# A down projection in pairs of column blocks, two of eight units by seven products

## The chip, the cores and the metric

The kernel runs on one core of one Trainium2 chip. The metric is the time of one execution on the device in microseconds (us); the time of a kernel is the median of its runs. The engines are called by their names or as the profile does: TensorE (PE; its weight loads PEld), VectorE (DVE), ScalarE (ACT), GpSimd (POOL) and SyncE (SP), whose queue issues the weight loads.

## The reference, cut to what matters

One decoder layer on 256 tokens of width 2048, in float32. The part that the change touches is the SwiGLU block with a hidden width of 5632:

```python
def swiglu(h, w_gate, w_up, w_down):
    g = jnp.einsum('bsd,df->bsf', h, w_gate)
    u = jnp.einsum('bsd,df->bsf', h, w_up)
    return jnp.einsum('bsf,fd->bsd', jax.nn.silu(g) * u, w_down)

h = layer_norm(ALPHA * h + m, ln1_g[i], ln1_b[i])
f = swiglu(h, w_ffn_gate[i], w_ffn_up[i], w_ffn_down[i])
h = layer_norm(ALPHA * h + f, ln2_g[i], ln2_b[i])
```

A mixer (a linear recurrence beside attention) comes ahead of it, and a gated per-layer input behind it.

## The kernel before

**Arithmetic.** Every float32 operand is split into a high part, a cast to fp32r, and a low part, the rest. A block product is three matmuls: high by high, high by low, low by high. The activations are the stationary operand (128 features by 128 tokens), the weights are the moving operand (128 features by 512 columns), and the sum builds up in a PSUM bank of 128 tokens by 512 columns, one for each half `h` of the tokens.

**Weights.** The class `Stream` brings the weights in, in the fixed order of the list `srcs`. A unit is one load of 128 x 2048 floats. SP's queue loads it (`load`, three units ahead at most); ScalarE casts the high part of a half of it (`prepare_hi`, line 156); VectorE subtracts to get the low part (`prepare_lo`, line 147). The halves rotate through six buffers, so a cast waits until TensorE has used up the half six places before. `free` says that a half is used up; `tick`, called after every six matmuls or so, runs the steps of other jobs that are due (each job is a Python generator, one step to a tick) and then prepares at most one low and one high part. No scheduler reorders anything: each engine works in the order in which the program issues.

**SwiGLU.** `FPARTS` cuts the hidden width into three parts of 16, 16 and 12 tiles of 128 features. A part is four (or three) groups of gate and up (`gate_up`, four tiles each), which leave the transposed product in `hT`, and then the part's down projection, added to the residual `z`.

In `gate_up` a unit is two feature tiles of the input by four column tiles of both gate and up. The first six units take eight block products each. The last two (`SEVEN`) take seven by Strassen's scheme: besides the four accumulators `q` there are `p1`, `p6`, `p5` and `p7`, the stationary operands of some products are sums of activations (`xsum`, made once in `sums_of_x1`), and the moving ones are sums of weights, which VectorE makes in `add_up` (line 128). Such a unit has four halves to prepare, one of them half as wide. `finish` puts the products together, applies silu and writes `hT` over some 18 ticks, well into the stage behind it.

In the down projection of before a unit is four tiles of `hT` by one column block of 512 columns. Blocks 0 and 1 run together, unit by unit, in four accumulators (`two`); block 2 and then block 3 follow by themselves, in two accumulators each. `token_major` issues a unit (lines 270 to 272 are the three matmuls); `residuals` adds a finished accumulator to `z` (lines 681 and 683) as a job, one token half to a tick. PSUM has four banks for these accumulators (tag `mm`), two more with the tag `aux` and two with the tag `sc`.

Of the kernel before, what the change touches and what calls it, by code (L numbers as in the profile page):

```python
# [20 lines left out]
P = 128  # L21
D = 2048
S = 256
KT = D // P
# [24 lines left out]
NSM = 32 + 8 * 4 + 1 + 64  # L49
PAIRS = KT // 2  # L50
SEVEN = 2


class Stream:
# [5 lines left out]

    def __init__(self, nc, pool, srcs, after_load, sevens):
        self.nc, self.pool, self.srcs, self.after_load = nc, pool, srcs, after_load
        self.sevens = sevens
        self.order = [(n, j) for n in range(len(srcs)) for j in range(4 if n in sevens else 2)]
        self.place = {key: i for i, key in enumerate(self.order)}
        self.sums, self.sums_pool = {}, None
        self.loaded = self.released = self.his = self.los = 0
        self.freed = self.seen = 0  # L70
        self.w32, self.parts, self.jobs, self.spare = {}, {}, [], []
        self.unit = 0
        self.held = False
# [22 lines left out]
    def load(self):  # L96
        while self.loaded < min(max(self.released, FIRST) + BUFS, len(self.srcs)):
            n = self.loaded
            w = self.new_load()
            if isinstance(self.srcs[n], tuple):  # L100
                for i, src in enumerate(self.srcs[n]):
                    dst = w[:, i * 1024:(i + 1) * 1024].rearrange("p (f c) -> p f c", f=4)
                    self.nc.sync.dma_start(dst, src)
            else:
                for c in (slice(0, 1024), slice(1024, 2048)) if n == FIRST else (slice(0, 2048),):
                    self.nc.sync.dma_start(w[:, c], self.srcs[n][:, c])
            if n in self.after_load:
                self.after_load[n]()

    def blocks(self, n):  # L110

        return self.w32[n].rearrange("p (g f k c) -> p g f k c", g=2, f=4, k=2)

    def source(self, i):

        n, j = self.order[i]
        if n in self.sevens and j:
            if j == 1:
                return self.blocks(n)[:, 1, :, 1, :], 512
            return self.sums[n][:, (j - 2) * 1024:(j - 1) * 1024], 1024  # L120
        return self.w32[n][:, j * 1024:j * 1024 + 1024], 1024

    def shaped(self, t, src, cols):
        return t[:, :cols].rearrange("p (f c) -> p f c", f=4) if cols == 512 else t

    def add_up(self, n, j):

        add = lambda out, a, b: self.nc.vector.tensor_tensor(out, a, b, ALU.add)
        b = self.blocks(n)
        if j == 0:  # L130
            self.sums[n] = self.sums_pool.tile([P, 2048], F32, tag="T", name="sums", bufs=2)
        t = self.sums[n].rearrange("p (i f c) -> p i f c", i=4, f=4)
        if j == 0:
            w = self.w32[n]
            diagonal = bass.AP(w.tensor, w.offset, [w.ap[0], [1024 + P, 2], [2 * P, 4], [1, P]])
            add(t[:, 0:2], diagonal, b[:, 1, :, 0, :].unsqueeze(1).broadcast_to([P, 2, 4, P]))
        else:
            t1, t2, t4 = t[:, 0], t[:, 2], t[:, 3]
            add(t2, t1, b[:, 1, :, 1, :])
            add(t4, t2, b[:, 0, :, 1, :])  # L140

    def prepare_lo(self):
        n, j = self.order[self.los]
        wh, wl = self.parts[n, j]
        src, cols = self.source(self.los)
        wh, wl = (self.shaped(t, src, cols) for t in (wh, wl))
        self.nc.vector.tensor_tensor(wl, src, wh.bitcast(F32), ALU.subtract)  # L147
        self.released += j == 1
        self.los += 1
        self.load()  # L150

    def prepare_hi(self):
        n, j = self.order[self.his]
        src, cols = self.source(self.his)
        wh, wl = self.new_half()
        self.nc.scalar.copy(self.shaped(wh, src, cols), src)  # L156
        if n in self.sevens and j < 2:
            self.add_up(n, j)

# [41 lines left out]
def tile_hybrid_layer(ctx: ExitStack, tc: tile.TileContext, t: dict):  # L201
# [14 lines left out]
    srcs += [t["w_out"][blk, kq] for blk, kq in OUT01]  # L216
    srcs += [t["w_out"][blk, kq] for blk in (2, 3) for kq in range(4)]
    srcs += [t["w_pp"][u] for u in range(2)]
    sevens = set()
    for f0, nf in FPARTS:  # L220
        for f in range(f0, f0 + nf, 4):
            sevens.update(range(len(srcs) + PAIRS - SEVEN, len(srcs) + PAIRS))
            srcs += [tuple(t[w][f:f + 4, :, 2 * P * j:2 * P * (j + 1)].rearrange("f p c -> p f c")
                           for w in ("w_gate", "w_up")) for j in range(PAIRS)]
        srcs += [t["w_down"][f0 // 4 + kq, blk] for kq in range(nf // 4) for blk in range(2)]
        srcs += [t["w_down"][f0 // 4 + kq, blk] for blk in range(2, 4) for kq in range(nf // 4)]
    srcs += [t["w_pg"][blk, kq] for blk in range(4) for kq in range(4)]
    after_load = {}
    st = Stream(nc, wp, srcs, after_load, sevens)

    def bank(name):
        return pm.tile([P, 512], F32, tag="mm", name=name)

    def aux(name):
        return pa.tile([P, 512], F32, tag="aux", name=name, bufs=2)
# [560 lines left out]
    x1 = act.tile([P, KT, 2 * S], F32R, tag="B", name="x1")  # L796
    xsum = []

    def sums_of_x1():

        xsum.append(late.tile([P, SEVEN, 4, 2, P], F32R, tag="gb", name="xsum"))
        work = act.tile([P, 2 * SEVEN * 512], F32, tag="A", name="work")
        x, sums = work[:, :SEVEN * 512], work[:, SEVEN * 512:]
        ks = slice(KT - 2 * SEVEN, KT)
        nc.vector.tensor_tensor(x.rearrange("p (k s) -> p k s", s=S), x1[:, ks, :S].bitcast(F32),
                                x1[:, ks, S:].bitcast(F32), ALU.add)
        yield
        a11, a21, a12, a22 = (x.rearrange("p (m i c) -> p m i c", i=4, c=P)[:, :, i, :] for i in range(4))  # L810
        s1, s3, s2, s4 = (sums.rearrange("p (m i c) -> p m i c", i=4, c=P)[:, :, i, :] for i in range(4))
        nc.vector.tensor_tensor(s1, a22, a21, ALU.subtract)
        nc.vector.tensor_tensor(s3, a11, a21, ALU.subtract)
        yield
        nc.vector.scalar_tensor_tensor(s2, s1, -1.0, a11, ALU.mult, ALU.subtract)
        nc.vector.tensor_tensor(s4, a12, s2, ALU.add)
        yield
        sums = sums.rearrange("p (n c) -> p n c", c=P)
        hi, lo = (xsum[0].rearrange("p m i a c -> p (m i) a c")[:, :, a, :] for a in range(2))
        nc.scalar.copy(hi, sums)  # L820
        yield
        nc.vector.tensor_tensor(lo, sums, hi.bitcast(F32), ALU.subtract)

    ps = [bank("ops") for _ in range(2)]
    for kq in range(2):
# [8 lines left out]

    def product(ps, a, w, first, last):

        out = ps.rearrange("p (f c) -> p f c", c=P)
        nc.tensor.matmul(out, a[0], w[0], start=first, stop=False)  # L838
        nc.tensor.matmul(out, a[0], w[1], start=False, stop=False)  # L839
        nc.tensor.matmul(out, a[1], w[0], start=False, stop=last)  # L840

    def operand(n, j, i):

        parts = st.half(n, j)
        if n in st.sevens and j:
            return [w[:, i * 512:(i + 1) * 512].rearrange("p (f c) -> p f c", c=P) for w in parts]
        return [w.rearrange("p (f k c) -> p f k c", f=4, k=2)[:, :, i, :] for w in parts]

    def gate_up(hT, i0):
# [46 lines left out]
    def finish(hT, i0, q, p1, p6, p5, p7):  # L896
# [34 lines left out]
        for h, g in enumerate((g0, g1)):  # L931
            tp = aux("tp")
            for i in range(4):
                nc.tensor.transpose(tp[:, i * P:(i + 1) * P], g[:, i * P:(i + 1) * P], ident)
            yield
            tp = tp.rearrange("p (a b) -> p a b", b=P)
            hi, lo = (hT[:, i0:i0 + 4, o + h * P:o + (h + 1) * P] for o in (0, S))
            nc.scalar.copy(hi, tp)
            yield
            nc.vector.tensor_tensor(lo, tp, hi.bitcast(F32), ALU.subtract)  # L940

    for part, (f0, nf) in enumerate(FPARTS):
        hT = None
        for i0 in range(0, nf, 4):
            hT = gate_up(hT, i0)
        nq = nf // 4
        end = part == len(FPARTS) - 1
        if end:
            gb = load_gb(2)
        two = [[bank("dps") for _ in range(2)] for _ in range(2)]  # L950
        for kq in range(nq):
            for blk in range(2):
# [187 lines left out]
```

## Time and profile before

| | |
|---|---|
| runs | 1183.46 us median of 3 (1183.11 to 1183.65) |
| profiled execution | 1183.25 us, of which the span of the trace is 1181.4 us |
| granted TensorE clock, mean | 0.996 |
| part 0: gate and up, then down projection | down from 530.0 to 618.7 us of the span |
| part 1: down projection | 790.3 to 878.9 us |

Times in the profile count from the start of the span. A line of the timeline gives the start, the duration and the instruction, and, in brackets, how long its engine stood idle in front of it and what ended that. The names are those of the program's tiles (`dps` is an accumulator of the down projection, `gu` and `p` those of gate and up, `wh` and `wl` high and low parts of weights).

### The profile page before, as it was taken

What the parts mean: (1) busy time and instruction counts of PE and PEld (TensorE: products, weight loads), DVE (VectorE), ACT (ScalarE), POOL (GpSimd) and SP (SyncE); (2) the same over time, 40 slices, a digit from 0 to 9 for tenths busy, and PEclk for the clock granted to TensorE, in tenths of its full rate; (3) what the DMA queues carried; (4) which work ended last, traced back from release to release, by engine and by line L of the source; (5) the groups of instructions that cost most, each with busy time, mean ns of one, the idle gap of its engine ahead of it and who ended that gap; (6) DMA issues with size and microseconds to landing.
All of it is one profiled execution on the core that took longest, in us unless ns stands there. A gap on an engine that the chain in (4) does not pass through costs nothing.

```text
span 1181.4 us, 14679 instructions
## 1 busy us (share of the span) xinstructions
PE 1163.0 (98%) x5576; PEld 967.3 (82%) x5576; DVE 871.7 (74%) x1126; ACT 629.1 (53%) x905; POOL 36.7 (3%) x64
## 2 busy tenths in 40 slices
PE   9999999999999999999999999999999999999995
PEld 6888888888888888888888888888888888877885
DVE  6965987775669877876555887885556887766877
ACT  6767566664356655654333664664334664535540
POOL 0000000001010000000000000000000000002001
PEclk9999999999999999999999999999999999999998
DMA  9766554547638557546565655655564755755741
GB/s 331 264 219 211 170 179 151 178 151 268 267 127 295 184 182 246 180 173 218 187 205 178 214 170 187 214 189 203 189 203 152 234 185 178 287 179 221 296 158 72
DMA packets 119703, 238.99 MB, mean 202 GB/s; under 512 B 5904, under 2 KB 100024, under 8 KB 103632
## 3 DMA queue, kind: packets, MB, share of 16 engines
q1 hardware_dynamic: 116208, 221.52, 54.7%
q0 software_dynamic: 3424, 16.53, 3.7%
q8 instruction: 44, 0.72, 0.2%
q14 instruction: 27, 0.22, 0.1%
HBM read 233.82 MB, written 5.78 MB: 203 GB/s over the span
## 4 chain that ended last, share of the span: by engine, by line
PE 95%; DVE 2%; ACT 1%; POOL 1%; DMA 0%; issue 0%; SPq 0%; DVEq 0%; POOLq 0%; ACTq 0%
PE gu L838 11%; PE gu L840 11%; PE gu L839 11%; PE dps L270 6%; PE dps L272 6%; PE dps L271 6%; PE q L244 3%; PE k L244 3%; PE yg L244 3%; PE ops L270 2%; PE ops L272 2%; PE ops L271 2%; PE xr L244 2%; PE gps L271 2%; PE gps L270 2%; PE gps L272 2%
## 5 line engine op out<-in xcount | busy, mean ns | idle before, releaser
L147 DVE TENSOR_TENSOR wl<-w,wh 128x1024 fp32r<-128x1024 f32 (+1 forms) x404 | 478.8, 1192 | 174.9 <-ACT wh L156 173.3
L156 ACT CAST wh<-w 128x1024 fp32r<-128x1024 f32 (+1 forms) x404 | 413.8, 1031 | 315.3 <-PE dps L272 120.2
L838 PE MATMUL gu<-wh,x 128*128 128x512 f32 x572 | 224.4, 392 | 0.0
L840 PE MATMUL gu<-wh,x 128*128 128x512 f32 x572 | 222.7, 389 | 0.0
L839 PE MATMUL gu<-wl,x 128*128 128x512 f32 x572 | 222.7, 389 | 0.0
L270 PE MATMUL dps<-wh,hT 128*128 128x512 f32 x352 | 138.0, 392 | 1.4 <-DVE z L683 1.1
L272 PE MATMUL dps<-wh,hT 128*128 128x512 f32 x352 | 137.1, 389 | 0.0
L271 PE MATMUL dps<-wl,hT 128*128 128x512 f32 x352 | 137.0, 389 | 0.0
L840 PEld LDWEIGHTS gu<-wh,x 128*128 128x128 f32 x572 | 107.4, 188 | 22.7
L838 PEld LDWEIGHTS gu<-wh,x 128*128 128x128 f32 x572 | 107.4, 188 | 21.8
L839 PEld LDWEIGHTS gu<-wl,x 128*128 128x128 f32 x572 | 107.5, 188 | 21.8
L147 DVE TENSOR_TENSOR wl<-sums,wh 128x1024 fp32r<-128x1024 f32 x44 | 52.9, 1224 | 49.5 <-ACT wh L156 49.5
L270 PEld LDWEIGHTS dps<-wh,hT 128*128 128x128 f32 x352 | 66.1, 188 | 16.4 <-issue 2.3
L272 PEld LDWEIGHTS dps<-wh,hT 128*128 128x128 f32 x352 | 66.1, 188 | 13.8
L271 PEld LDWEIGHTS dps<-wl,hT 128*128 128x128 f32 x352 | 66.1, 188 | 13.4
L156 ACT CAST wh<-sums 128x1024 fp32r<-128x1024 f32 x44 | 45.2, 1051 | 50.0 <-PE gu L840 41.9
L270 PE MATMUL ops<-wh,mhl 128*128 128x512 f32 x128 | 50.4, 394 | 0.0
L271 PE MATMUL ops<-wl,mhl 128*128 128x512 f32 x128 | 49.9, 390 | 0.0
L272 PE MATMUL ops<-wh,mhl 128*128 128x512 f32 x128 | 49.9, 390 | 0.0
L244 PE MATMUL xr<-xhl,wh 128*128 128x512 f32 x128 | 45.9, 401 | 1.6 <-ACT wh L76 1.6
L244 PE MATMUL q<-xhl,wh 128*128 128x512 f32 x128 | 47.3, 406 | 0.0
L244 PE MATMUL k<-xhl,wh 128*128 128x512 f32 x128 | 46.0, 400 | 0.0
(250 smaller groups left out, 1771.4 us busy)
## 6 DMA issues: line engine op xcount, KB each, us to landing
w<-in_w_gate SPq DMA_DIRECT2D x88, 512.0 KB, 3.7
w<-in_w_up SPq DMA_DIRECT2D x88, 512.0 KB, 4.8
w<-in_w_down SPq DMA_DIRECT2D x44, 1024.0 KB, 4.8
w<-in_w_a SPq DMA_DIRECT2D x28, 1024.0 KB, 4.9
w<-in_w_out SPq DMA_DIRECT2D x16, 1024.0 KB, 4.9
w<-in_w_pg SPq DMA_DIRECT2D x16, 1024.0 KB, 4.9
w<-in_w_v SPq DMA_DIRECT2D x8, 1024.0 KB, 4.9
gb<-in_ln_g POOLq DMA_DIRECT2D x3, 1024.0 KB, 5.2
```

The lines of the kernel that those rows point to most:

```text
L147: self.nc.vector.tensor_tensor(wl, src, wh.bitcast(F32), ALU.subtract)
L156: self.nc.scalar.copy(self.shaped(wh, src, cols), src)
L244: nc.tensor.matmul(ps, wh[:, c], xhl[:, k, :], start=(k == 0), stop=False)
L270: nc.tensor.matmul(ps, ah, wh[:, c], start=first, stop=False)
L271: nc.tensor.matmul(ps, ah, wl[:, c], start=False, stop=False)
L272: nc.tensor.matmul(ps, al, wh[:, c], start=False, stop=last)
L838: nc.tensor.matmul(out, a[0], w[0], start=first, stop=False)
L839: nc.tensor.matmul(out, a[0], w[1], start=False, stop=False)
L840: nc.tensor.matmul(out, a[1], w[0], start=False, stop=last)
```

## The change

In parts 0 and 1 the down projection goes by pairs of column blocks. A unit is now two tiles of `hT` (`m` counts these pairs of tiles) by two column blocks, 8 units to a pair, in the order of `DOWN`. Kind "N" is a unit of eight block products, kind "S" one of seven. The four accumulators of a pair (two token halves by two column blocks) run through all eight units, and each is read into `z` right after its own last product. The S units need sums of `hT`'s first four tiles, made behind the first group of gate and up of the part (`sums_of`), and their weights' sums (`add_up`); `p1`, `p6`, `p5` and `p7` run over both S units of a pair, and `products_to_z` adds them to `z` in nine additions. Weights come as two loads of 512 KB to a unit. Part 2 is as before.

```diff
+DOWN = ((("N", 2), ("N", 3), ("N", 4), ("N", 5), ("S", 0), ("N", 6), ("S", 1), ("N", 7)),
+        (("N", 2), ("N", 3), ("N", 4), ("S", 0), ("N", 5), ("N", 6), ("S", 1), ("N", 7)))
...
+        if nf == KT:
+            for pair, order in enumerate(DOWN):
+                for kind, m in order:
+                    if kind == "S":
+                        sevens.add(len(srcs))
+                    plain.add(len(srcs))
+                    srcs.append(tuple(t["w_down"][f0 // 4 + m // 2, 2 * pair + i, :, m % 2 * 1024:m % 2 * 1024 + 1024]
+                                      for i in range(2)))
+            continue
...
-        xsum.append(late.tile([P, SEVEN, 4, 2, P], F32R, tag="gb", name="xsum"))
+        xsum.append(late.tile([P, 2 * SEVEN, 4, 2, P], F32R, tag="gb", name="xsum"))
...
             nc.vector.tensor_tensor(lo, tp, hi.bitcast(F32), ALU.subtract)
+        if i0 == 0 and paired:
+            yield
+            yield from sums_of(hT, 0, late.tile([P, 2048], F32, tag="T", name="work", bufs=2), SEVEN)
+
+    def down_pair(hT, pair, order, scale):
+
+        n0 = st.take(len(order))
+        q = [[bank("dps") for _ in range(2)] for _ in range(2)]
+        places = [i for i, (kind, _) in enumerate(order) if kind == "S"]
+        for pos, (kind, m) in enumerate(order):
+            n, end = n0 + pos, pos == len(order) - 1
+            first, last = pos == places[0], pos == places[-1]
+            def x(h, i):
+                return [hT[:, 2 * m + i, o + h * P:o + (h + 1) * P] for o in (0, S)]
+            def sx(i):
+                return [xsum[0][:, SEVEN + m, i, a, :] for a in range(2)]
+            if kind == "N":
+                for g in range(2):
+                    for h in range(2):
+                        for i in range(2):
+                            product(q[h][g], x(h, i), operand(n, g, i), pos + i == 0, end and i == 1)
+                        if end:
+                            residual(h, 2 * pair + g, q[h][g], scale)
+                        st.free(h)
+                        st.tick()
+                continue
+            if first:
+                p1, p6 = aux("p1"), aux("p6")
+                both = pa.tile([P, 2, 512], F32, tag="sc", name="p57")
+                p5, p7 = both[:, 0, :], both[:, 1, :]
+            product(q[0][0], x(0, 1), operand(n, 0, 1), False, False)
+            product(p1, x(0, 0), operand(n, 0, 0), first, last)
+            st.free()
+            st.tick()
+            product(q[0][1], sx(3), operand(n, 1, 0), False, False)
+            st.free()
+            product(p5, sx(0), operand(n, 2, 0), first, last)
+            st.tick()
+            product(p7, sx(1), operand(n, 2, 1), first, last)
+            st.free()
+            product(q[1][0], x(1, 1), operand(n, 3, 1), False, False)
+            st.tick()
+            product(p6, sx(2), operand(n, 3, 0), first, last)
+            if last:
+                st.start(products_to_z(pair, p1, p6, p5, p7))
+            st.free()
+            st.tick()
+
+    def products_to_z(pair, p1, p6, p5, p7):
+
+
+        add = lambda out, a, b, op=ALU.add: nc.vector.tensor_tensor(out, a, b, op)
+        c1, u2, u3, u4 = (tmp(i) for i in ("c1", "u2", "u3", "u4"))
+        nc.scalar.copy(c1, p1)
+        yield
+        add(u2, p6, c1)
+        yield
+        add(u3, p7, u2)
+        yield
+        add(u2, p5, u2)
+        yield
+        add(u4, p5, u3)
+        yield 2
+        for h, g, u, op in ((0, 0, c1, ALU.add), (1, 0, u3, ALU.add), (0, 1, u2, ALU.subtract),
+                            (1, 1, u4, ALU.subtract)):
+            c = slice((2 * pair + g) * 512, (2 * pair + g + 1) * 512)
+            add(z[:, h, c], z[:, h, c], u, op)
+            yield
...
+        if paired:
+            for pair, order in enumerate(DOWN):
+                down_pair(hT, pair, order, part == 0)
+            continue
         two = [[bank("dps") for _ in range(2)] for _ in range(2)]
```

`sums_of` is the body of the old `sums_of_x1` with its source, its place in `xsum` and its work buffer as arguments: one addition of 1024 columns, four of 256, a cast and a subtraction of 1024. In `Stream`, the units in `plain` are read as two column blocks of two tiles of 512 columns in a row, where those of gate and up have four pieces of 128 columns.

## Rows read from the trace of the kernel before

**Rows 1.** The page: span, then busy us (share) and instructions of each engine.
```profile
span 1181.4 us, 14679 instructions
...
PE 1163.0 (98%) x5576; PEld 967.3 (82%) x5576; DVE 871.7 (74%) x1126; ACT 629.1 (53%) x905; POOL 36.7 (3%) x64
```

**Rows 2.** TensorE's waits, whole span: for whom, us, times, longest.
```profile
PE dps L270 <- DVE z L683: 1.1, 3, 0.4
PE dps L270 <- DVE z L681: 0.4, 1, 0.4
```

**Rows 3.** TensorE's timeline, part 0's down projection: start us, us, instruction.
```profile
530.01 0.39 PE L270 MATMUL dps<-wh,hT 128*128 128x512 f32 x1
...
543.38 0.39 PE L272 MATMUL dps<-wh,hT 128*128 128x512 f32 x1
```

**Rows 4.** The same timeline at the step to the third column block.
```profile
574.30 0.39 PE L272 MATMUL dps<-wh,hT 128*128 128x512 f32 x1
575.06 0.47 PE L270 MATMUL dps<-wh,hT 128*128 128x512 f32 x1 [0.38 <-DVE z L681]
575.37 0.40 PE L271 MATMUL dps<-wl,hT 128*128 128x512 f32 x1
```

**Rows 5.** The same step in part 1.
```profile
834.56 0.39 PE L272 MATMUL dps<-wh,hT 128*128 128x512 f32 x1
835.33 0.47 PE L270 MATMUL dps<-wh,hT 128*128 128x512 f32 x1 [0.38 <-DVE z L683]
```

**Rows 6.** VectorE's timeline at the step of rows 4.
```profile
573.09 1.23 DVE L147 TENSOR_TENSOR wl<-w,wh 128x1024 fp32r<-128x1024 f32 x1 [1.50 <-ACT wh L156]
574.23 1.28 DVE L681 SCALAR_TENSOR_TENSOR z<-z,dps 128x512 f32<-128x512 f32 x2
```

**Rows 7.** Busy time by stretch: a gate and up group, part 0's down projection.
```profile
core 0: us, PE busy (x) PEld busy (x) DVE busy (x) ACT busy (x) POOL busy (x), PEclk, DMA share, GB/s
444.40:487.50 43.10, 43.10 (x195) 35.70 (x194) 34.67 (x39) 23.97 (x30) 0.00 (x0) 1.00 0.59 194
530.00:618.67 88.67, 88.29 (x393) 72.80 (x392) 51.83 (x52) 37.37 (x39) 0.00 (x0) 1.00 0.59 206
```

**Rows 8.** Groups by shape on VectorE: count | busy us, mean ns | idle before.
```profile
L147 DVE TENSOR_TENSOR wl<-w,wh 128x1024 fp32r<-128x1024 f32 x382 | 463.8, 1222 | 174.9 <-ACT wh L156 173.3
...
L128 DVE TENSOR_TENSOR sums<-sums,w 128x512 f32<-128x512 f32 x44 | 30.3, 689 | 0.8
...
L899 DVE TENSOR_TENSOR u<-p,u 128x512 f32<-128x512 f32 x44 | 30.2, 686 | 0.4
...
L128 DVE TENSOR_TENSOR sums<-w 128x1024 f32<-128x1024 f32 x22 | 26.8, 1219 | 0.7 <-DMA w<-in_w_up 0.7
...
L147 DVE TENSOR_TENSOR wl<-w,wh 128x512 fp32r<-128x512 f32 x22 | 15.1, 684 | 0.0
...
L683 DVE TENSOR_TENSOR z<-z,dps 128x512 f32<-128x512 f32 x16 | 10.5, 679 | 3.1 <-PE dps L272 3.1
...
L77 DVE TENSOR_TENSOR wl<-w,wh 128x256 fp32r<-128x256 f32 x21 | 7.7, 421 | 0.4 <-ACT wh L76 0.4
```

**Rows 9.** TensorE's timeline, the last two units of a gate and up group.
```profile
477.34 0.39 PE L838 MATMUL gu<-wh,x 128*128 128x512 f32 x1
...
484.14 0.39 PE L838 MATMUL p<-wh,xsum 128*128 128x512 f32 x1
...
486.86 0.39 PE L838 MATMUL gu<-wh,x 128*128 128x512 f32 x1
```

**Rows 10.** VectorE's timeline in the same group, subtractions from the sums.
```profile
470.51 1.23 DVE L147 TENSOR_TENSOR wl<-sums,wh 128x1024 fp32r<-128x1024 f32 x1 [2.32 <-ACT wh L156]
...
480.03 2.36 DVE L147 TENSOR_TENSOR wl<-sums,wh 128x1024 fp32r<-128x1024 f32 x2 [0.92 <-ACT wh L156]
```

**Rows 11.** The page: DMA issues, count, KB each, median us to landing.
```profile
w<-in_w_gate SPq DMA_DIRECT2D x88, 512.0 KB, 3.7
...
w<-in_w_down SPq DMA_DIRECT2D x44, 1024.0 KB, 4.8
```

More of the change, by code (lines that the diff above doesn't have):

```diff
@@ L51, with __init__ @@
 SEVEN = 2
+DOWN = ((("N", 2), ("N", 3), ("N", 4), ("N", 5), ("S", 0), ("N", 6), ("S", 1), ("N", 7)),
+        (("N", 2), ("N", 3), ("N", 4), ("S", 0), ("N", 5), ("N", 6), ("S", 1), ("N", 7)))
 class Stream:
-    def __init__(self, nc, pool, srcs, after_load, sevens):
+    def __init__(self, nc, pool, srcs, after_load, sevens, plain):
+        self.plain = plain
         self.nc, self.pool, self.srcs, self.after_load = nc, pool, srcs, after_load
@@ L101, in load @@
                 for i, src in enumerate(self.srcs[n]):
-                    dst = w[:, i * 1024:(i + 1) * 1024].rearrange("p (f c) -> p f c", f=4)
+                    dst = w[:, i * 1024:(i + 1) * 1024]
+                    dst = dst if n in self.plain else dst.rearrange("p (f c) -> p f c", f=4)
                     self.nc.sync.dma_start(dst, src)
@@ L110, in blocks @@
     def blocks(self, n):
-        return self.w32[n].rearrange("p (g f k c) -> p g f k c", g=2, f=4, k=2)
+        if n in self.plain:
+            return self.w32[n].rearrange("p (g k c) -> p g k c", g=2, k=2)
+        return self.w32[n].rearrange("p (g f k c) -> p g k f c", g=2, f=4, k=2)
     def source(self, i):
@@ L118, in source, with shaped @@
             if j == 1:
-                return self.blocks(n)[:, 1, :, 1, :], 512
+                return self.blocks(n)[:, 1, 1], 512
             return self.sums[n][:, (j - 2) * 1024:(j - 1) * 1024], 1024
         return self.w32[n][:, j * 1024:j * 1024 + 1024], 1024
-    def shaped(self, t, src, cols):
-        return t[:, :cols].rearrange("p (f c) -> p f c", f=4) if cols == 512 else t
+    def shaped(self, t, n, cols):
+        if cols == 1024 or n in self.plain:
+            return t[:, :cols]
+        return t[:, :cols].rearrange("p (f c) -> p f c", f=4)
     def add_up(self, n, j):
@@ L131, in add_up @@
             self.sums[n] = self.sums_pool.tile([P, 2048], F32, tag="T", name="sums", bufs=2)
-        t = self.sums[n].rearrange("p (i f c) -> p i f c", i=4, f=4)
+        w = self.w32[n]
+        if n in self.plain:
+            t = self.sums[n].rearrange("p (i c) -> p i c", i=4)
+            diagonal = bass.AP(w.tensor, w.offset, [w.ap[0], [1024 + 512, 2], [1, 512]])
+            b12 = b[:, 1, 0].unsqueeze(1).broadcast_to([P, 2, 512])
+        else:
+            t = self.sums[n].rearrange("p (i f c) -> p i f c", i=4, f=4)
+            diagonal = bass.AP(w.tensor, w.offset, [w.ap[0], [1024 + P, 2], [2 * P, 4], [1, P]])
+            b12 = b[:, 1, 0].unsqueeze(1).broadcast_to([P, 2, 4, P])
         if j == 0:
-            w = self.w32[n]
-            diagonal = bass.AP(w.tensor, w.offset, [w.ap[0], [1024 + P, 2], [2 * P, 4], [1, P]])
-            add(t[:, 0:2], diagonal, b[:, 1, :, 0, :].unsqueeze(1).broadcast_to([P, 2, 4, P]))
+            add(t[:, 0:2], diagonal, b12)
         else:
             t1, t2, t4 = t[:, 0], t[:, 2], t[:, 3]
-            add(t2, t1, b[:, 1, :, 1, :])
-            add(t4, t2, b[:, 0, :, 1, :])
+            add(t2, t1, b[:, 1, 1])
+            add(t4, t2, b[:, 0, 1])
     def prepare_lo(self):
@@ L145, in prepare_lo @@
         src, cols = self.source(self.los)
-        wh, wl = (self.shaped(t, src, cols) for t in (wh, wl))
+        wh, wl = (self.shaped(t, n, cols) for t in (wh, wl))
         self.nc.vector.tensor_tensor(wl, src, wh.bitcast(F32), ALU.subtract)
@@ L155, in prepare_hi @@
         wh, wl = self.new_half()
-        self.nc.scalar.copy(self.shaped(wh, src, cols), src)
+        self.nc.scalar.copy(self.shaped(wh, n, cols), src)
         if n in self.sevens and j < 2:
@@ L218, in tile_hybrid_layer @@
     srcs += [t["w_pp"][u] for u in range(2)]
-    sevens = set()
+    sevens, plain = set(), set()
     for f0, nf in FPARTS:
@@ L228, in tile_hybrid_layer @@
     after_load = {}
-    st = Stream(nc, wp, srcs, after_load, sevens)
+    st = Stream(nc, wp, srcs, after_load, sevens, plain)
     def bank(name):
@@ L797, in tile_hybrid_layer, with sums_of @@
     xsum = []
-    def sums_of_x1():
-        xsum.append(late.tile([P, SEVEN, 4, 2, P], F32R, tag="gb", name="xsum"))
-        work = act.tile([P, 2 * SEVEN * 512], F32, tag="A", name="work")
+    def sums_of(xt, k0, work, m0):
         x, sums = work[:, :SEVEN * 512], work[:, SEVEN * 512:]
-        ks = slice(KT - 2 * SEVEN, KT)
-        nc.vector.tensor_tensor(x.rearrange("p (k s) -> p k s", s=S), x1[:, ks, :S].bitcast(F32),
-                                x1[:, ks, S:].bitcast(F32), ALU.add)
+        ks = slice(k0, k0 + 2 * SEVEN)
+        nc.vector.tensor_tensor(x.rearrange("p (k s) -> p k s", s=S), xt[:, ks, :S].bitcast(F32),
+                                xt[:, ks, S:].bitcast(F32), ALU.add)
         yield
@@ L818, in sums_of_x1 @@
         sums = sums.rearrange("p (n c) -> p n c", c=P)
-        hi, lo = (xsum[0].rearrange("p m i a c -> p (m i) a c")[:, :, a, :] for a in range(2))
+        hi, lo = (xsum[0][:, m0:m0 + SEVEN].rearrange("p m i a c -> p (m i) a c")[:, :, a, :] for a in range(2))
         nc.scalar.copy(hi, sums)
@@ L822, in sums_of_x1 @@
         nc.vector.tensor_tensor(lo, sums, hi.bitcast(F32), ALU.subtract)
+    def sums_of_x1():
+        xsum.append(late.tile([P, 2 * SEVEN, 4, 2, P], F32R, tag="gb", name="xsum"))
+        work = act.tile([P, 2 * SEVEN * 512], F32, tag="A", name="work")
+        yield from sums_of(x1, KT - 2 * SEVEN, work, 0)
     ps = [bank("ops") for _ in range(2)]
@@ L835, in product @@
     def product(ps, a, w, first, last):
-        out = ps.rearrange("p (f c) -> p f c", c=P)
+        out = ps.rearrange("p (f c) -> p f c", c=P) if len(w[0].shape) == 3 else ps
         nc.tensor.matmul(out, a[0], w[0], start=first, stop=False)
@@ L844, in operand @@
         parts = st.half(n, j)
-        if n in st.sevens and j:
-            return [w[:, i * 512:(i + 1) * 512].rearrange("p (f c) -> p f c", c=P) for w in parts]
+        if n in st.plain or n in st.sevens and j:
+            return [w[:, i * 512:(i + 1) * 512] for w in parts]
         return [w.rearrange("p (f k c) -> p f k c", f=4, k=2)[:, :, i, :] for w in parts]
@@ L942, in tile_hybrid_layer @@
     for part, (f0, nf) in enumerate(FPARTS):
-        hT = None
+        hT, paired = None, nf == KT
         for i0 in range(0, nf, 4):
```

## The prediction, as it was made

> **What bounds the kernel now.** I read the page's busy shares first [rows 1]: TensorE is at work in 98% of the span, VectorE in 74%. A busy share alone doesn't say that TensorE sets the pace, because its matmul records overlap, so I went to TensorE's own waits next. There are hardly any: in the down projections of the three parts together it waited 1.5 us in four places, each time for VectorE to take a sum out of an accumulator [rows 2]. The stages of part 0 and part 1 run at the granted clock 1.00, the upper level, 2.4 GHz [rows 7]. So in the stretch that the change touches the end is set by how many matmuls TensorE is given, and by nothing else except two short waits.
>
> The price of one matmul has to be read from starts, not from durations. In part 0's down projection the first matmul starts at 530.01 and the sixtieth at 543.38 [rows 3]: 13.37 us over 59 steps, 0.2266 us each. A record's own duration is 0.39 us; whoever multiplies by that counts the overlap twice and gets a gain 1.7 times too large.
>
> The two waits are at the step from the second to the third block of columns. In part 0 the last matmul of block 1 starts at 574.30, the next at 575.06 and the one behind it at 575.37 [rows 4]: 1.07 us for two steps that should take 0.45, so 0.62 lost. Part 1 shows the same gap, 834.56 to 835.33 [rows 5], and I put it at the same 0.62. The reason stands on VectorE: the readout of block 0's accumulator (z, line 681) comes to its turn at 574.23, straight behind a 1.23 us weight subtraction [rows 6], though block 0 itself had been finished a whole unit earlier.
>
> **The change part by part.**
>
> *Removed: matmuls.* A unit is 2 tiles of the 16 by 2 column blocks by 2 token halves: 8 block products of 3 matmuls, 24, or 5.44 us. An S unit has 7 products, 21 matmuls, 4.76 us. Eight S units (2 of 8 in each of 2 pairs of 2 parts) save 24 matmuls: 24 x 0.2266 = 5.44 us. That the seven products keep the same step is seen in gate and up, where the scheme is in use: the last two units of a group, 42 matmuls, run from 477.34 to 486.86 [rows 9], 9.52 us, again 0.2267 each, with the four extra accumulators in play. The operand of a plain unit is 512 columns in a row, as that of the old down projection.
>
> By the Trainium skill ("TensorE: Matmul & The Clock Gate", Back-to-back issue gap) a stream of weight loads and matmuls of 512 columns sustains about 131 ns for one, and an isolated one about 216 ns. By these the saving would be an estimated 3.1 or 5.2 us; the row shows 0.2266 us over 59 steps without a break, and the row decides.
>
> *Moved: the readout of accumulators.* Four accumulators now run through a whole pair and each is read right behind its own last product, in program order ahead of that step's weight preparation. The next user of the same accumulator comes 18 matmuls, 4.08 us, after its last product. A readout takes 0.68 us [rows 8]. I take the two waits of 0.62 as gone: 1.24 us. Lower bound of this term: they stay or come back at all four pair ends (rival B). Upper bound: there is nothing more than these to win here.
>
> *Added on VectorE, per S unit.* Subtractions: three of 1024 columns and one of 512 in place of two of 1024, 3 x 1.22 + 0.68 = 4.35 against 2.44. Sums: one of 1.22 and two of 0.69, 2.60. Together 6.95 us where a plain unit has 2.44 [rows 8]. *Per pair:* nine 512-column additions from the four extra accumulators into z, 9 x 0.69 = 6.2, of the kind of line 899. *Per part:* the sums of hT in the second group of gate and up: 1.22 + 4 x 0.42 + 1.22 = 4.1, the 256-column ones by the row of line 77. For the down projection of one part that is 4 x 4.51 + 2 x 6.2 = 30.4 on top of 51.8 [rows 7]: 82.2 of the 85.3 us that the stage will then last (88.67 less 12 x 0.2266 and 0.62). This is 96%, and the one thing that speaks against the change.
>
> I cost it at nothing, and the cover is this. Six halves of weights are prepared ahead of TensorE, so work on VectorE delays nothing until that lead is eaten. In program order the densest stretch of a pair is from one step into the first S unit to two steps behind its end: subtractions and sums for the second S unit, 1.22 + 1.22 + 1.22 + 1.38 + 0.68 + 1.22 + 1.22 = 8.2 us at full durations, while TensorE spends 6.1 us. VectorE comes out 2 us late, but the first of these halves is wanted a whole plain unit, 5.4 us, after the S unit ends, and the last 3.4 us later still. In pair 1 the additions into z fall together with the first S unit's sums (about 8.5 us against 6.8), and that unit is still one and a half plain units away. In gate and up two S units stand side by side, a harder case: there VectorE idled 2.32 us in front of the first of these subtractions, and the last two, done by 482.4 [rows 10], were first wanted at 484.14 [rows 9], 1.7 us or more later. VectorE is busy 34.67 of 43.10 us there [rows 7], so the 4.1 us of hT sums go into a group with 8.4 idle. If no lead were left, each S unit would cost TensorE 6.95 - 4.76 = 2.2 us (rival C).
>
> *ScalarE, loads.* An S unit has casts of 1024, 512, 1024 and 1024 columns in place of two; ScalarE is busy 37.37 of 88.67 us in this stage [rows 7]: no bound. Each weight load is two of 512 KB in place of one of 1024 KB, 32 more issues on SP's queue. Loads of 512 KB land 3.7 us after issue, those of 1024 KB 4.8 us [rows 11], and they are issued three units ahead; the stage's DMA share is 0.59. Nothing.
>
> *What queues behind what.* The readouts at a pair's end wait at the head of VectorE's queue for TensorE, and weight subtractions and the additions of the extra products stand behind them. From the end of the second S unit, counted in us: readout of the first accumulator 1.4 to 2.0, addition to 2.7, subtraction to 4.0; second readout to 4.6, addition and subtraction to 6.5; third to 7.2, addition to 7.9; fourth to 8.6. TensorE wants these accumulators again at 5.4, 6.8, 8.2 and 9.5. The least slack is 0.9 us.
>
> *Sum.* 5.44 + 1.24 = 6.68 us. The profiled execution took 1183.25 us, 1.85 outside its span of 1181.4 and 0.21 below the median of the runs; the saving lies inside the span, so 1183.46 - 6.68 = 1176.8 us, 0.56% faster.
>
> **The rivals.**
>
> *B: the accumulators still hold TensorE.* The slack of 0.9 us is less than one subtraction of 1.22; if one more lands in that stretch, each of four pair ends pays about what the step paid before, 0.62. Then 1176.8 + 4 x 0.62 = 1179.3 us. For it: the wait of before came about in just this way, a readout behind a subtraction [rows 6]. Against it: the readout is now issued ahead of that step's subtraction.
> By the Trainium skill ("TensorE: Matmul & The Clock Gate", the table of specifications) VectorE's queue is strictly first in, first out. The trace agrees: the readout at 574.23 began only as the subtraction of 573.09 let it.
>
> *C: VectorE becomes the bound, slower.* Place: the S units of the down projection. If the waits on casts don't shrink as VectorE fills up, the lead drains and each of eight S units lasts as long as VectorE's 6.95 us: 8 x 2.19 = 17.5, so 1194.3 us. It turns the gain into a loss from 6.68 / 4 = 1.7 us of TensorE waiting per pair. For it: 82.2 of 85.3 us. Against it: gate and up carry two S units and ten 512-column operations of their own in 43.1 us and TensorE has no wait there [rows 2].
>
> *D: the hT sums fall on the path.* They use the buffers in which the weight sums rotate, in the group where VectorE has least room. In full, 2 x 4.1 = 8.2: 1185.0 us, no change that could be told. Against it: 8.4 us idle in that group, 2.32 of it right behind the place of the sums [rows 7, 10].
>
> **How the numbers follow.** The forecast 0.80 (1176.0 to 1178: the runs lie 0.3 to either side of their median, and a pair end or two may keep a wait), B 0.11, C 0.05, D 0.04. This kernel's runs tell a change from none at about 0.2%, 2.4 us. Faster: forecast and B, 0.91; same: D, 0.04; slower: C, 0.05. The range runs from 1176.0 to B's end, 1179.3.
>
> **What would show it.** In part 0's down projection 372 matmuls where 384 stood, 85.3 us from its first to the first of the next gate and up; steps of 0.2266 us through the S units and over all four pair ends; no wait of TensorE for z in parts 0 and 1; VectorE near 80 us busy in the stage, with idle time in front of subtractions mostly gone. Wrong would be: gaps on TensorE ended by wl (C) or by sums (D), or by z at pair ends (B); a step longer than 0.2266 in S units would undo the first term itself.

## The result, and the profile after

The changed kernel takes 1176.32 us (median of 6 runs, 1175.78 to 1177.56), where the kernel before took 1183.45 (6 runs beside it). The ratio is 0.9942, with a 95% interval of 0.9931 to 0.9953: 7.13 us or 0.6% less, where 6.68 were forecast and 1176.8 us.

The page's span and busy times, which answer to [rows 1]: TensorE has 24 matmuls fewer and VectorE 57 us more work.

```profile
span 1174.0 us, 14815 instructions
...
PE 1156.7 (99%) x5552; PEld 963.5 (82%) x5552; DVE 928.4 (79%) x1210; ACT 644.7 (55%) x927; POOL 36.8 (3%) x64
```

TensorE's timeline at the edges of the two down projections: the first matmul of each, and the first of the gate and up group behind it (product is now line 867).

```profile
529.24 0.39 PE L867 MATMUL dps<-wh,hT 128*128 128x512 f32 x1
...
614.55 0.39 PE L867 MATMUL gu<-wh,x 128*128 128x512 f32 x1
...
786.16 0.39 PE L867 MATMUL dps<-wh,hT 128*128 128x512 f32 x1
...
871.47 0.39 PE L867 MATMUL gu<-wh,x 128*128 128x512 f32 x1
```

Part 0's stage lasts 614.55 - 529.24 = 85.31 us, part 1's 871.47 - 786.16 = 85.31, where 88.66 stood between the same edges before. That is 3.35 us each, 6.70 together, against 6.68 worked out. The stage holds the 372 matmuls of the 16 units that were worked out; the row of it below counts 381, with eight transposes of gate and up and one matmul that began ahead of it. In the profiled runs the span fell by 7.4. What it fell beyond the stages lies ahead of part 0's first gate and up, which comes before any work that the change adds: 0.79 us. The first matmul there in the trace of before, and now:

```profile
358.31 0.48 PE L838 MATMUL gu<-wh,x 128*128 128x512 f32 x1
...
357.52 0.48 PE L867 MATMUL gu<-wh,x 128*128 128x512 f32 x1
```

All of TensorE's waits over the whole span, which answer to [rows 2]. The first three lie outside the down projections of parts 0 and 1; the last, line 296, is the unchanged down projection of part 2. None is left in parts 0 and 1.

```profile
PE tp L748 <- ACT z L742: 1.5, 2, 1.3
PE xr L270 <- ACT wh L81: 1.2, 2, 0.7
PE wps L334 <- DVE zero L331: 1.2, 1, 1.2
PE dps L296 <- DVE z L709: 0.7, 2, 0.4
```

VectorE's timeline, the four readouts at the first pair's end:

```profile
568.51 0.69 DVE L707 SCALAR_TENSOR_TENSOR z<-z,dps 128x512 f32<-128x512 f32 x1 [1.26 <-PE dps L869]
...
570.85 0.68 DVE L707 SCALAR_TENSOR_TENSOR z<-z,dps 128x512 f32<-128x512 f32 x1
...
573.18 0.68 DVE L707 SCALAR_TENSOR_TENSOR z<-z,dps 128x512 f32<-128x512 f32 x1
...
574.38 0.68 DVE L707 SCALAR_TENSOR_TENSOR z<-z,dps 128x512 f32<-128x512 f32 x1
```

And TensorE's timeline, the first matmul of the next pair in each of the same four accumulators:

```profile
572.39 0.39 PE L867 MATMUL dps<-wh,hT 128*128 128x512 f32 x1
...
573.75 0.39 PE L867 MATMUL dps<-wh,hT 128*128 128x512 f32 x1
...
575.11 0.39 PE L867 MATMUL dps<-wh,hT 128*128 128x512 f32 x1
...
576.47 0.39 PE L867 MATMUL dps<-wh,hT 128*128 128x512 f32 x1
```

The readouts end at 569.20, 571.53, 573.86 and 575.06. The slack is 3.2, 2.2, 1.25 and 1.4 us; the prediction's count by hand had 0.9 as the least. VectorE stood idle 1.26 us in front of the first readout, waiting for TensorE.

The busy times by stretch, by the columns of [rows 7]. The group of gate and up in [rows 7] is the third, and the sums of hT are made in the second, so this is the second group, in the kernel before and now, and then the down projection of part 0:

```profile
core 0: us, PE busy (x) PEld busy (x) DVE busy (x) ACT busy (x) POOL busy (x), PEclk, DMA share, GB/s
400.59:443.71 43.12, 43.12 (x195) 35.71 (x194) 34.84 (x39) 25.30 (x31) 0.00 (x0) 1.00 0.61 197
...
399.79:442.94 43.15, 43.15 (x196) 35.70 (x194) 38.41 (x45) 26.24 (x32) 0.00 (x0) 1.00 0.60 196
...
529.24:614.55 85.31, 85.31 (x381) 70.62 (x380) 70.99 (x80) 44.23 (x49) 0.00 (x0) 1.00 0.65 207
```

VectorE is busy 70.99 of 85.31 us, not the 82.2 that the prediction put together. The second group of gate and up has the six instructions of the sums of hT, 3.57 us more of VectorE, and lasts 43.15 us where it lasted 43.12.

### The profile page after: what moved, and what is told of

Its sections match the earlier page's. It is cut to its first block, busy times and chain, and to the rows that moved or that the text cites. A ratio compares the mean times of both kernels' runs of the same rounds, so it can differ in the third digit from the quotient of the medians.

```text
span 1174.0 us, 14815 instructions
## 1 busy us (share of the span) xinstructions
PE 1156.7 (99%) x5552; PEld 963.5 (82%) x5552; DVE 928.4 (79%) x1210; ACT 644.7 (55%) x927; POOL 36.8 (3%) x64
## 4 chain that ended last, share of the span: by engine, by line
PE 95%; DVE 2%; POOL 1%; ACT 1%; DMA 0%; issue 0%; SPq 0%; DVEq 0%; POOLq 0%; ACTq 0%
PE gu L867 12%; PE gu L868 12%; PE gu L869 11%; PE dps L868 4%; PE dps L867 4%; PE dps L869 4%; PE q L270 3%; PE k L270 3%; PE yg L270 3%; PE ops L296 2%; PE ops L298 2%; PE ops L297 2%; PE xr L270 2%; PE p L868 2%; PE p L867 2%; PE p L869 2%
## 5 line engine op out<-in xcount | busy, mean ns | idle before, releaser
L164 DVE TENSOR_TENSOR wl<-w,wh 128x1024 fp32r<-128x1024 f32 (+1 forms) x404 | 473.8, 1181 | 113.4 <-ACT wh L173 111.3
L173 ACT CAST wh<-w 128x1024 fp32r<-128x1024 f32 (+1 forms) x404 | 409.4, 1023 | 274.0 <-PE gu L869 99.6
L164 DVE TENSOR_TENSOR wl<-sums,wh 128x1024 fp32r<-128x1024 f32 x60 | 72.1, 1222 | 45.2 <-ACT wh L173 45.2
L173 ACT CAST wh<-sums 128x1024 fp32r<-128x1024 f32 x60 | 62.1, 1052 | 65.2 <-PE gu L869 36.8
L867 PE MATMUL dps<-wh,hT 128*128 128x512 f32 x208 | 81.3, 391 | 0.0
L869 PE MATMUL dps<-wh,hT 128*128 128x512 f32 x208 | 81.0, 389 | 0.0
L868 PE MATMUL dps<-wl,hT 128*128 128x512 f32 x208 | 81.0, 389 | 0.0
L270 PE MATMUL yg<-xhl,wh 128*128 128x512 f32 x128 | 46.0, 399 | 0.0
L869 PEld LDWEIGHTS dps<-wh,hT 128*128 128x128 f32 x208 | 39.1, 188 | 8.2
L867 PEld LDWEIGHTS dps<-wh,hT 128*128 128x128 f32 x208 | 39.1, 188 | 8.1
```

Of the source, the lines that this page charges most:

```text
L173: self.nc.scalar.copy(self.shaped(wh, n, cols), src)
L270: nc.tensor.matmul(ps, wh[:, c], xhl[:, k, :], start=(k == 0), stop=False)
```

## The experiments

Times are medians of the runs; the edges of the down projection, read as above, are the sharper measure, since the stretch ahead of part 0's down projection lasted between 528.95 and 530.56 us in the profiles of the changed kernel and of the ten runs below. A ratio is against the kernel before in runs beside that experiment on the same chip, with its 95% interval; not all experiments ran on one chip, and the kernel before took 1183.30 to 1184.11 us there.

**The changed kernel again**

> The changed kernel as it is, on the same chip as the three beside it: 1176.3 us, the down projection of parts 0 and 1 lasting 85.31 us each, whatever the time up to the first of them is (that differed by 1.3 us between profiles).

No edit. It took 1177.55 us (1175.99 to 1178.11), ratio 0.9944 (0.9931 to 0.9958). Both stages lasted 85.31 us: to the hundredth what they lasted in the first profile, while the median moved by 1.2, on a chip where the kernel before takes 1184.11 us. What follows therefore goes by the stages.

**All units plain**

```diff
-DOWN = ((("N", 2), ("N", 3), ("N", 4), ("N", 5), ("S", 0), ("N", 6), ("S", 1), ("N", 7)),
-        (("N", 2), ("N", 3), ("N", 4), ("S", 0), ("N", 5), ("N", 6), ("S", 1), ("N", 7)))
+DOWN = (tuple(("N", m) for m in range(8)),) * 2
...
-        if i0 == 0 and paired:
+        if False:
...
```

> All eight units of every pair take eight products; the pairs, the readouts and the loads stay as changed. The theory (24 matmuls are worth 5.44 us, the two vanished waits 1.24 us) expects 1183.45 - 1.24 = 1182.2 us. The rival that the new staging, not the seven products, brought the gain expects about 1176.3. The rival that staging by pairs costs something which the seven products pay for expects 1183.5 or more.

It took 1182.14 us (1180.74 to 1182.67), ratio 0.9991 (0.9982 to 1.0000). TensorE's timeline at the edges of part 0's down projection:

```profile
530.38 0.39 PE L866 MATMUL dps<-wh,hT 128*128 128x512 f32 x1
...
618.41 0.39 PE L866 MATMUL gu<-wh,x 128*128 128x512 f32 x1
```

88.03 us: 0.63 less than before, with no wait in the stage, and 2.72 more than with the seven products. So per part the new staging is worth 0.63 and the seven products 2.72, which is 12 x 0.2267. Both terms of the sum are as worked out, and the rivals (all by the staging; or the staging costs something) fall.

**Readouts started behind the pair**

```diff
-                        if end:
-                            residual(h, 2 * pair + g, q[h][g], scale)
                         st.free(h)
                         st.tick()
...
+        for g in range(2):
+            st.start(residuals(2 * pair + g, [q[0][g], q[1][g]], scale), 1 + 2 * g)
...
         add(u4, p5, u3)
-        yield 2
+        yield 6
```

> The changed kernel with the four readouts of a pair started as jobs behind the pair's last unit, as the kernel before did it, and the nine additions' last four moved four ticks back. The theory (the place of the readout in VectorE's order is what made TensorE wait) expects at least 0.62 us at each of four pair ends: 1178.8 us or more, with TensorE waiting for z. The rival (four accumulators for a whole pair leave time enough wherever the readout stands) expects 1176.3.

It took 1182.86 us (1182.10 to 1183.56), ratio 0.9997 (0.9988 to 1.0006). By the runs the whole gain is given back, by the stages below 6.09 of the 6.70 us. TensorE's timeline at the end of the first pair:

```profile
572.24 0.39 PE L869 MATMUL dps<-wh,hT 128*128 128x512 f32 x1
573.93 0.47 PE L867 MATMUL dps<-wh,hT 128*128 128x512 f32 x1 [1.30 <-DVE z L707]
```

VectorE's timeline there:

```profile
570.77 1.28 DVE L1021 TENSOR_TENSOR u<-p,u 128x512 f32<-128x512 f32 x2
571.97 1.22 DVE L164 TENSOR_TENSOR wl<-w,wh 128x1024 fp32r<-128x1024 f32 x1
573.10 1.28 DVE L707 SCALAR_TENSOR_TENSOR z<-z,dps 128x512 f32<-128x512 f32 x2
```

The first accumulator was complete four microseconds before 572.24, but its readout stands behind two additions and a subtraction and begins at 573.10. The stages last 88.36 and 88.35 us, 3.05 more per part and 1.5 for each pair end. The direction is the theory's, the size 2.5 times what I gave as its least: VectorE's queue is now fuller at this place than it was in [rows 6].

The Trainium skill ("TensorE: Matmul & The Clock Gate", the table of specifications) has VectorE's queue as strictly first in, first out; this run agrees: the readout began at 573.10, with the end of the last of the three instructions ahead of it (573.19 by its record).

**Readout one place further back**

```diff
-                        if end:
-                            residual(h, 2 * pair + g, q[h][g], scale)
                         st.free(h)
                         st.tick()
+                        if end:
+                            residual(h, 2 * pair + g, q[h][g], scale)
```

> The changed kernel with each pair-end readout issued just behind its step's weight preparation, not ahead of it: VectorE does one subtraction of 1.14 us first. In the trace of the changed kernel the readouts end 1.2 to 3.2 us ahead of the next use. The theory (only slack counts) expects no wait or at most 0.1 us at a pair end: 1176.3 us. The rival (being ahead of that subtraction is what the change owes its missing waits to) expects about 0.6 at each of four pair ends: 1178.8.

It took 1176.55 us (1176.18 to 1178.62), ratio 0.9939 (0.9926 to 0.9951), with both stages at 85.31. VectorE's timeline, the readouts of the first pair:

```profile
570.21 0.68 DVE L707 SCALAR_TENSOR_TENSOR z<-z,dps 128x512 f32<-128x512 f32 x1
...
572.54 0.68 DVE L707 SCALAR_TENSOR_TENSOR z<-z,dps 128x512 f32<-128x512 f32 x1
...
573.74 0.68 DVE L707 SCALAR_TENSOR_TENSOR z<-z,dps 128x512 f32<-128x512 f32 x1
...
576.07 0.68 DVE L707 SCALAR_TENSOR_TENSOR z<-z,dps 128x512 f32<-128x512 f32 x1
```

They end 1.0 to 2.8 us ahead of the next use, which in this profile is at 573.64 and then every 1.36. What counts is that the readout is issued within the pair, not that it is ahead of that one subtraction, which here takes the place of the idle time in front of the first readout.

**Without the sums of hT and the additions into z**

```diff
-                return [xsum[0][:, SEVEN + m, i, a, :] for a in range(2)]
+                return [xsum[0][:, m, i, a, :] for a in range(2)]
...
-        if i0 == 0 and paired:
+        if False:
...
-        nc.scalar.copy(c1, p1)
...
-            add(z[:, h, c], z[:, h, c], u, op)
-            yield
+        for u, ps in ((c1, p1), (u2, p6), (u3, p7), (u4, p5)):
+            nc.scalar.copy(u[:, :8], ps[:, :8])
+            yield
```

> The changed kernel without the sums of hT (the S units take sums of x1 in their place) and without the nine additions of the extra products into z (four copies of 8 columns read them instead), so that the extra products are left out of the result. 33 us of VectorE's work are gone. The theory (this work is fully covered) expects 1176.3 us within 0.4. The rival (VectorE's work falls on the path at the pair ends or in the second group of gate and up) expects 1175 or less, in the extreme 8 us less for the sums alone.

It took 1176.62 us (1176.06 to 1177.05), ratio 0.9943 (0.9930 to 0.9955). The row of its down projection in part 0, by the columns shown above:

```profile
530.56:615.88 85.32, 85.32 (x382) 70.62 (x381) 66.39 (x71) 43.98 (x55) 0.00 (x0) 1.00 0.64 206
```

Over the span VectorE has 44 instructions fewer (1166 against 1210) and is busy 903.1 us against 928.4, 25.3 us less where 33 were expected. The 44 are two times six for the sums of hT and four times eight for the extra products: they are eight additions to a pair, not nine as the part on the change, the prediction and the expectations have it. TensorE's stage is 85.32 us against 85.31, and the second group of gate and up, now without the sums, lasts 43.12 us against 43.15. This work costs nothing that could be told.

**Subtractions of the S units twice**

```diff
-        self.nc.vector.tensor_tensor(wl, src, wh.bitcast(F32), ALU.subtract)
+        for _ in range(2 if n in self.plain and n in self.sevens else 1):
+            self.nc.vector.tensor_tensor(wl, src, wh.bitcast(F32), ALU.subtract)
```

> The changed kernel with each weight subtraction of the down projection's S units done twice: 4.35 us more of VectorE per S unit, 17.4 per part, on 71.0 busy of 85.3. The theory (only the sum over a stage counts, since six halves of lead carry a dense stretch) expects VectorE full at 85 to 88 us per part and the time within 1176.3 to 1181. The rival (each S unit lasts as long as VectorE's own work for it, no lead) expects 8 x (11.3 - 4.76) = 52 us more, 1228.

It took 1179.73 us (1179.25 to 1180.45), ratio 0.9969 (0.9958 to 0.9980). Its row by the same columns:

```profile
529.83:616.35 86.52, 86.08 (x382) 70.39 (x381) 85.70 (x94) 43.85 (x49) 0.00 (x0) 1.00 0.61 193
```

VectorE is busy 85.70 of 86.52 us, yet TensorE lost only 1.21 us in the stage, in short gaps at three places. VectorE's timeline at the longest of them:

```profile
574.64 1.22 DVE L165 TENSOR_TENSOR wl<-w,wh 128x1024 fp32r<-128x1024 f32 x1
575.77 0.68 DVE L708 SCALAR_TENSOR_TENSOR z<-z,dps 128x512 f32<-128x512 f32 x1
```

The third readout now ends at 576.45, and TensorE, which was ready for its accumulator at 576.1, goes on at 576.60. 4.35 us more of VectorE in each S unit were worth nothing like the 52 us of the rival without a lead.

**S units side by side behind the pair end**

```diff
-        (("N", 2), ("N", 3), ("N", 4), ("S", 0), ("N", 5), ("N", 6), ("S", 1), ("N", 7)))
+        (("N", 2), ("S", 0), ("S", 1), ("N", 3), ("N", 4), ("N", 5), ("N", 6), ("N", 7)))
...
-        yield 2
+        yield 18 if pair else 2
```

> The changed kernel with the two S units of the second pair side by side in places 1 and 2, right behind the pair end (their additions into z as late as before, behind the readouts). The count of matmuls and VectorE's sum over the stage stay. The theory that only VectorE's sum over a stage counts expects 1176.3 us. The theory that the place counts, because sums, subtractions, readouts and the extra products' additions of the first pair meet in one stretch with less work of TensorE in it, expects a wait as in the run with three and four, 1.8 us or a little less per part: 1178.5 to 1180.

It took 1180.39 us (1179.79 to 1182.25), ratio 0.9970 (0.9960 to 0.9981), 0.4 above the range expected. Its row by the same columns:

```profile
530.28:617.41 87.13, 86.09 (x381) 70.39 (x380) 73.45 (x83) 44.01 (x49) 0.00 (x0) 1.00 0.63 203
```

VectorE has 13.7 us to spare in the stage and TensorE waits all the same, 1.82 us per part. TensorE's timeline inside the second S unit:

```profile
585.16 0.40 PE L867 MATMUL dps<-wh,xsum 128*128 128x512 f32 x1
586.43 0.50 PE L868 MATMUL dps<-wl,xsum 128*128 128x512 f32 x1 [0.87 <-DVE wl L164]
```

VectorE's timeline, from the last idle time ahead of it:

```profile
564.57 3.72 DVE L164 TENSOR_TENSOR wl<-w,wh 128x1024 fp32r<-128x1024 f32 x3 [1.37 <-ACT wh L173]
...
568.21 1.22 DVE L139 TENSOR_TENSOR sums<-w 128x1024 f32<-128x1024 f32 x1
...
585.69 0.68 DVE L164 TENSOR_TENSOR wl<-w,wh 128x512 fp32r<-128x512 f32 x1
...
586.29 2.35 DVE L164 TENSOR_TENSOR wl<-sums,wh 128x1024 fp32r<-128x1024 f32 x2
```

From 568.21 to past 586.29 VectorE runs all but without a break (sums for two S units, their subtractions, four readouts, eight additions), and the half-width subtraction that TensorE needs at 585.4 begins at 585.69. The theory that only the stage's sum counts falls. It also has to fit stretch by stretch, within the six halves. Standing side by side isn't enough for a wait: in the first pair of the runs with three, below, S units 0 and 1 stand side by side too, away from the readouts, and TensorE doesn't wait.

**Three S units of eight, sums used twice**

```diff
+DOWN = ((("N", 3), ("N", 4), ("N", 5), ("S", 0), ("S", 1), ("N", 6), ("S", 2), ("N", 7)),
+        (("N", 3), ("N", 4), ("S", 0), ("N", 5), ("S", 1), ("N", 6), ("S", 2), ("N", 7)))
...
-                return [xsum[0][:, SEVEN + m, i, a, :] for a in range(2)]
+                return [xsum[0][:, SEVEN + m % 2, i, a, :] for a in range(2)]
...
-        if i0 == 0 and paired:
+        if i0 in (0, 4) and paired:
             yield
-            yield from sums_of(hT, 0, late.tile([P, 2048], F32, tag="T", name="work", bufs=2), SEVEN)
+            yield from sums_of(hT, i0, late.tile([P, 2048], F32, tag="T", name="work", bufs=2), SEVEN)
```

> Three of eight units of a pair take seven products (the third with the activation sums of the first, so its part of the result is not the reference's), with a second set of activation sums made in the third group of gate and up so that VectorE's work is the full one. 12 more matmuls saved: the theory (TensorE's count sets the time while VectorE's work fits the stage) expects 1176.3 - 2.7 = 1173.6 us. By full durations VectorE has 9 us more per part, about 80 of 83.9. The rival (VectorE is already at its limit) expects 1176.3 or more.

It took 1174.33 us (1173.61 to 1175.64), ratio 0.9927 (0.9913 to 0.9940). Its row:

```profile
530.29:614.25 83.96, 83.96 (x376) 69.48 (x374) 78.52 (x90) 47.18 (x53) 0.00 (x0) 1.00 0.66 210
```

The stages last 83.96 and 83.95 us, some 1.36 less than 85.31 each: six matmuls, as the theory has it, and no wait in them. The time is 0.7 above the 1173.6 expected, outside these stages.

**Three and four S units**

The edit is against the run with three.

```diff
-        (("N", 3), ("N", 4), ("S", 0), ("N", 5), ("S", 1), ("N", 6), ("S", 2), ("N", 7)))
+        (("N", 4), ("S", 0), ("S", 1), ("N", 5), ("S", 2), ("N", 6), ("S", 3), ("N", 7)))
```

> As the run with three, with four of eight units in the second pair of each part (same sums used twice, so not the reference's result). 18 matmuls fewer than the changed kernel: the theory with the lead that carries VectorE's lateness into the following group expects 1176.3 - 4.1 = 1172.2 us. VectorE's work in the second pair, at back-to-back spacing some 43 us, is above TensorE's 40.8; if the lead does not carry it, the pair lasts 2 us longer, and the time is 1176 or more.

It took 1175.64 us (1175.50 to 1176.36), ratio 0.9936 (0.9924 to 0.9949). Its row:

```profile
529.51:614.56 85.05, 84.01 (x372) 68.70 (x371) 82.50 (x95) 48.19 (x55) 0.00 (x0) 1.00 0.64 207
```

TensorE's timeline where it waits longest:

```profile
583.71 0.40 PE L867 MATMUL dps<-wh,xsum 128*128 128x512 f32 x1
...
584.98 0.50 PE L868 MATMUL dps<-wl,xsum 128*128 128x512 f32 x1 [0.88 <-DVE wl L164]
```

85.31 less nine matmuls would be 83.27; it is 85.05. The missing 1.78 are waits for subtractions in the second S unit of the second pair, at the place and of the size (1.82) that the run with two side by side shows, so the place alone accounts for them, and the 1172.2 expected was missed. That the load of the fourth unit would have been free elsewhere isn't shown: VectorE had 2.5 us to spare over the stage, but ran all but without idle time from 563.11 to 609.41, through nearly all of the second pair:

```profile
563.11 3.72 DVE L164 TENSOR_TENSOR wl<-w,wh 128x1024 fp32r<-128x1024 f32 x3 [0.58 <-ACT wh L173]
...
610.68 0.69 DVE L707 SCALAR_TENSOR_TENSOR z<-z,dps 128x512 f32<-128x512 f32 x1 [1.27 <-PE dps L869]
```

Four units spread out weren't tried.

**Three S units with sums of their own**

```diff
-    phl = late.tile([P, 2, 2 * S], F32R, name="phl")
+    phl = late.tile([P, 2, 2 * S], F32R, tag="phl", name="phl")
...
+        if i0 == 4 and paired:
+            yield
+            third.append(late.tile([P, 1, 4, 2, P], F32R, tag="phl", name="third"))
+            yield from sums_of(hT, 4, late.tile([P, 2048], F32, tag="T", name="work", bufs=2), third[-1], 1)
...
-                return [xsum[0][:, SEVEN + m, i, a, :] for a in range(2)]
+                return [(xsum[0][:, SEVEN + m, i, a, :] if m < SEVEN else third[-1][:, 0, i, a, :]) for a in range(2)]
```

with `DOWN` as in the run with three.

> Three of eight units of a pair take seven products, the third with activation sums of its own, kept in the place of a tile that is no longer used by then. The whole reference is computed. The theory expects the down projection of a part to last 83.95 us, as in the run with three, so 12 matmuls or 2.72 us less than the changed kernel: 1173.6 us, with no wait of TensorE in parts 0 and 1. The rival (the gain of the third unit is given back by VectorE) expects 1176.3.

It took 1173.91 us (1172.78 to 1174.59), ratio 0.9912 (0.9899 to 0.9926). Its row:

```profile
528.95:612.90 83.95, 83.95 (x375) 69.48 (x374) 78.48 (x90) 47.16 (x53) 0.00 (x0) 1.00 0.66 210
```

The stages last 83.95 and 83.94 us, with no wait for VectorE in them. This version beats both kernels: 2.73 us of stage less than the changed one.

## Why the prediction was right

*The matmul's price.* 24 x 0.2266 = 5.44 us was worked out; with and without the seven products the stages differ by 2 x 2.72 = 5.44. The start-to-start step held through all S units.

*The two waits.* 1.24 us was taken as gone; the run with plain units alone gives 2 x 0.63 = 1.26. That no wait came back at the pair ends is due to readouts issued inside the pair: started behind it, they cost 1.5 us an end. My reason against rival B, that the readout stands ahead of that step's subtraction, was not what saved it: one subtraction earlier or later changed nothing. Rival B had left out that VectorE waits for TensorE there, 1.26 us, and one more subtraction fits into that. My price for B, 0.62, was too small for the worse order and would have been right for none that was run.

*VectorE's cover.* Costed at nothing, and nothing it was: leaving out the additions into z moved the stage by 0.01 us; the group that makes the hT sums lasts 43.12 us without them and 43.15 with them, which excludes D's 4.1 us a part; TensorE has no wait for VectorE in these stages, which excludes C for this order. The load itself was mis-sized, 82.2 us against 70.99. The sum has 38 more instructions in the stage, one addition too many in each of two pairs, and the trace has 28 more (80 against 52): the other eight, six additions and one more readout of the second pair and one subtraction, fall outside the stage's edges. The ten are worth 7.4 us. The rest, 3.8 us, is that instructions issued back to back overlap: of two 1024-column subtractions of 1.22 us the second starts 1.14 us behind the first.

*The loads.* Put at nothing on a landing time of 3.7 us for 512 KB [rows 11], which is that of one of two kinds of 512 KB load. The other kind before, and the loads of the changed down projection:

```profile
w<-in_w_up SPq DMA_DIRECT2D x88, 512.0 KB, 4.8
...
w<-in_w_down SPq DMA_DIRECT2D x64, 512.0 KB, 5.1
```

So the landing time was read too short; TensorE has no wait in the stages, and the term is nothing all the same.

*The lead of six halves.* The densest stretch was worked through for the order as written, and came out 2 us late on VectorE, with more than that in hand. The trace bears it out. VectorE's last subtractions for the second S unit of the first pair, and the ones behind its next idle time:

```profile
558.66 2.35 DVE L164 TENSOR_TENSOR wl<-sums,wh 128x1024 fp32r<-128x1024 f32 x2
...
563.52 3.73 DVE L164 TENSOR_TENSOR wl<-w,wh 128x1024 fp32r<-128x1024 f32 x3 [1.37 <-ACT wh L173]
```

TensorE's first matmul of that unit:

```profile
562.19 0.39 PE L867 MATMUL dps<-wh,hT 128*128 128x512 f32 x1
```

All four low parts are done at 561.01, before the unit begins, and VectorE then has idle time again. That the order had to be worked through shows in the run with two S units side by side behind the pair end: the same sums, 1.82 us lost per part. Rival C's mechanism exists; what it needs is not a full stage but a full stretch.

*The sum.* The stages gave 6.70 of the forecast 6.68. The rest of the measured 7.13 is within the spread of the runs and of the stretch ahead of part 0's first gate and up.

## What to carry to other kernels

Where TensorE sets the pace, price a removed matmul by the step from start to start, and read the gain stage by stage: edges agree to 0.01 us where medians of the same kernel move by 1 us. Work that is to hide on another engine has to fit in its densest stretch and not only in the stage: list that engine's instructions in issue order between two deadlines, and spread the extra units away from readouts. As long as both fit, take the next unit too; here three of eight were as free as two.

## What was not expected

After each wait TensorE's next step is longer as well, 0.31 us in place of 0.23 in [rows 4] and 0.30 to 0.34 at the gaps of the other runs, so a wait costs 0.07 to 0.11 more than its gap. The stretch up to part 0's down projection lasted from 528.95 to 530.56 us. All of that spread is there when the first gate and up of part 0 begins, at 357.25 to 358.86, ahead of all work that the change or an edit adds or takes away; from there to the down projection all runs, and the kernel before, take 171.69 to 171.75 us. What moves the start was not followed up.
